# Attention by whole heads with a late division, and part of an output projection moved among the mixers

## The chip, the cores and the metric

The kernel runs on one core of one Trainium2 chip. The metric is the device time of one execution in microseconds. In the profile PE is TensorE's matmul, PEld its weight load, DVE is VectorE, ACT is ScalarE, POOL is GpSimd, SP is SyncE, which issues the DMAs.

## What is computed

Two transformer blocks of two layers each, over 512 tokens of 1024 features, in fp32. Only the second block's token mixing is touched. In one layer of it three mixers read the same normalised input, and their outputs, side by side, go through one output projection:

```python
h = rms_norm_2(x, norm_g[l, 0]) * (1.0 + sc1) + sh1
aq, ak, av, bq, bff, bfb, bi, bg, cq, ck, cv = jnp.split(h @ w_in[l], split_idx, axis=-1)
o_a = mixer_a(...)            # softmax attention, 6 heads of 64, 2 key heads
o_b = mixer_b(...)            # gated linear recurrence in both directions, 4 heads
o_c = mixer_c(...)            # attention with a bias by distance, 6 heads, 2 key heads
mix = jnp.concatenate([o_a, o_b, o_c], axis=-1) @ w_out[l]     # 384 + 256 + 384 -> 1024
x = x + g1 * mix
h = rms_norm_2(x, norm_g[l, 1]) * (1.0 + sc2) + sh2
x = x + g2 * conv_ffn(h, ...)
```

An attention head's output is `softmax(q k^T) v`: exponentials of the scores, divided by their row sums, times the values.

## The kernel before, in words

Activations lie with features on the partitions: a tensor of 1024 features by 512 tokens is eight tiles of 128 x 512. Each weight matrix is cut into tiles of 128 output features. To keep fp32 precision, a product is done as three matmuls on rounded halves (high x high, high x low, low x high): `wload` fetches a raw weight tile, ScalarE rounds it (`wh`, L141), VectorE takes the remainder (`wl`, L146), and `mm3` (L186) issues the three. Two buffers each hold the raw, the high and the low weights.

The mixers of one layer are Python generators, each of which yields an estimate of its TensorE time. `weave` draws from several of them: the next step comes from the stream with the smallest ratio of time so far to its weight. That gives each instruction its place in the program; a scheduler with a timeline simulation then orders each engine's instructions by readiness and that place. At run time every engine works in the order so fixed.

Mixer a and mixer c are attentions. `attn2_unit` takes two blocks of 128 queries of one head: scores for 512 keys (`s`, L1267), a pass of VectorE that copies them to `E` and takes the row maximum (L1376, L1438), ScalarE's exponential with the row sum (L1380, L1444), the reciprocal of the sums (L1383, L1445), and `normalise` (L607), which scales every row of `E`. Then `pv_out` transposes `E` by 128 x 128 blocks into PSUM (`pt`, L595), ScalarE copies that to `pT` (L597), and the product with the values is collected in `pv` (L600), the two query blocks in two halves of the partitions, each instruction 128 columns wide. VectorE copies it to `y` (L603). Two heads share one tile `y`.

Mixer b goes by pairs of heads. `b_levels` builds a triangular 512 x 512 matrix in nine levels of doubling block size: products of VectorE (`zz`, L1571, and `Y`, L1526), exponentials on ScalarE, a running sum on GpSimd (L1530), and small matmuls (`lv`, L1503, L1550, L1558). `b_out` multiplies it by the values (`pvb`), `b_norm` and `b_gate` finish.

A first `weave` runs b's first preparation beside a's. A second runs `b_levels(0)` beside a's attentions and c's first preparation. A third runs pair 1 of b, c's attentions (weight 22) and a chain of b's output, c's remaining preparation, b's norms and gates (weight 28). `room` marks the end of that chain: only from there on are finished `y` rounded into `oh` and `ol` (`mix_done`), since the tiles they take are in use until the last input projection.

Then `block2` loads the residual `x` from DRAM (L1774), where it was put before the mixers, and does the output projection: for each of eight output tiles a weight tile of 1024 columns and 24 matmuls over the eight tiles of `oh`, `ol` (`residual`, L1726, adds to `x`). The first three output tiles are done over 512 tokens, the last five first over tokens 0 to 255, then, as cover for the next norm, over tokens 256 to 511. The norm's chain is: squares on ScalarE, sums on VectorE, a column sum on TensorE (`stat`, L234), an inverse root in eleven small steps on GpSimd (L206 to L224), a broadcast by TensorE (`stat`, L239), scaling, and the two halves `hh` and `hl`. The feed-forward part (`up`) follows.

Of the kernel before, what the change touches and what calls it, by code (L numbers as in the profile page):

```python
# [16 lines left out]
P = 128  # L17
# [86 lines left out]
class Kern:  # L104
# [1153 lines left out]
    def attn2_unit(self, q, ks, v, kv, soft, finish, y, row, i0):  # L1258


        nc = self.nc
        es = []
        for j in range(2):
            i = i0 + j
# [4 lines left out]
            soft(s, i, j, e)  # L1269
# [97 lines left out]
    def a_units(self):  # L1367
        nc = self.nc
        for h in range(6):
            if h % 2 == 0:  # L1370
                y = self.b2("y")
            for i0 in (0, 2):
                mx, nm, sm, rc = (self.small(2) for _ in range(4))

                def soft(ps, i, j, e):
                    nc.vector.tensor_tensor_reduce(e, ps, bc(self.zero[:, 0:1], S), op0=ALU.add, op1=ALU.max, scale=1.0,  # L1376
                                                   scalar=-3e38, accum_out=mx[:, j:j + 1])
                    c = 8 * (h // 2) + 2 * i + h % 2
                    nc.vector.tensor_tensor(nm[:, j:j + 1], mx[:, j:j + 1], self.ansc[:, c:c + 1], op=ALU.mult)
                    nc.scalar.activation(e, e, AF.Exp, bias=nm[:, j:j + 1], scale=self.asc[:, c:c + 1], accum_out=sm[:, j:j + 1])  # L1380
# [6 lines left out]
                self.attn2_unit(self.aqs[h], self.aks[h // 3], self.va, h // 3, soft, finish, y, (h % 2) * 64, i0)  # L1387
                yield 2.6
            if h % 2:
                self.y2[h // 2] = y  # L1390
# [34 lines left out]
    def c_units(self):  # L1425
        nc = self.nc
        for h in range(6):
# [4 lines left out]
            if h % 2 == 0:  # L1432
                y = self.b2("y")
            for i0 in (0, 2):
                mx, nm, sm, rc = (self.small(2) for _ in range(4))

                def soft(ps, i, j, e):
                    nc.vector.tensor_tensor_reduce(e, ps, tb[:, 384 - P * i:896 - P * i], op0=ALU.add, op1=ALU.max, scale=1.0,  # L1438
                                                   scalar=-3e38, accum_out=mx[:, j:j + 1])

                def finish(es):
                    nc.vector.tensor_scalar(nm, mx, -1.0, None, op0=ALU.mult)
                    for j, e in enumerate(es):
                        nc.scalar.activation(e, e, AF.Exp, bias=nm[:, j:j + 1], accum_out=sm[:, j:j + 1])  # L1444
                    nc.vector.reciprocal(rc, sm)  # L1445
                    for j, e in enumerate(es):
                        self.normalise(e, rc[:, j:j + 1])

                self.attn2_unit(self.cqs[h], self.cks[h // 3], self.cva, h // 3, soft, finish, y, (h % 2) * 64, i0)
                yield 2.6  # L1450
            if h % 2:
                self.mix_done(5 + h // 2, y)
# [182 lines left out]
    def mixers(self):  # L1635
# [277 lines left out]
```

## Time and profile before

| | us |
|---|---|
| median of 3 runs | 3018.26 (3018.15 to 3021.32) |
| the profiled execution | 3018.07 |
| its span | 3016.3 |
| TensorE busy | 2910.5 (96%) |
| VectorE busy | 1921.0 (64%) |
| ScalarE busy | 1351.2 (45%) |
| chain that ended last: share on TensorE | 83% |

The span runs from the first to the last instruction of the profile. Busy time of TensorE counts each matmul from its issue to its modelled end, and matmuls overlap, so a busy TensorE isn't one that works at its peak. Stages of one layer repeat in the other: the second block's first layer lies at about 1650 to 2310 us, its second from there to the end.

### The profile page before, as it was taken

To read this page: it belongs to the slowest core of one execution; us is meant where nothing else is said; L and a number is where in the kernel's file an instruction comes from. 1 tells how busy PE (TensorE), PEld (TensorE's weight loads), DVE (VectorE), ACT (ScalarE), POOL (GpSimd) and SP (SyncE) were. 2 spreads that over 40 slices of the span, in tenths; PEclk is the share of its full clock that TensorE was granted. 3 is DMA by queue.
4 is the path that set the end of the run, shared out by engine and by line. 5 is a ranking of instruction groups with operands and counts; after the bars stand their busy time and mean duration, and the time that the engine had idled before them with its cause. 6 is when DMAs were issued, how large, how long until landed. Compare 5 with 4: busy or idle time off the path is not lost.

```text
span 3016.3 us, 46253 instructions
## 1 busy us (share of the span) xinstructions
PE 2910.5 (96%) x17942; PEld 2415.4 (80%) x17942; DVE 1921.0 (64%) x3731; ACT 1351.2 (45%) x2417; POOL 249.8 (8%) x492
## 2 busy tenths in 40 slices
PE   7999999999998999999999999999999998999999
PEld 5888888888887888777778776788888876788887
DVE  5565655555556566665666777688853788576642
ACT  3445454322235345653225675544433676454421
POOL 0000000001112000000112222000000223000000
PEclk9999999999998999999999998999999999999999
DMA  6221111333342323124664211355543311232233
GB/s 228 87 67 60 48 63 64 121 127 120 119 161 84 125 83 107 52 69 169 222 216 134 70 50 47 99 175 196 203 144 109 103 43 60 79 105 98 98 102 95
DMA packets 113164, 331.77 MB, mean 110 GB/s; under 512 B 18160, under 2 KB 20720, under 8 KB 112944
## 3 DMA queue, kind: packets, MB, share of 16 engines
q1 hardware_dynamic: 112944, 328.81, 32.9%
q8 instruction: 141, 2.31, 0.3%
q14 instruction: 79, 0.65, 0.1%
HBM read 300.51 MB, written 17.76 MB: 106 GB/s over the span
## 4 chain that ended last, share of the span: by engine, by line
PE 83%; DVE 8%; ACT 2%; issue 1%; DMA 1%; POOL 1%; SPq 0%; DVEq 0%; ACTq 0%; POOLq 0%
PE mm L186 31%; PE up L186 15%; PE dn L186 10%; PE pu L186 5%; PE pv L600 4%; PE pt L595 4%; PE po L186 3%; PE s L907 2%; PE pre L186 1%; PE s L624 1%; PE s L1267 1%; DVE zz L1571 1%; DVE wl L146 1%; PE pq L186 1%; DVE E L607 1%
## 5 line engine op out<-in xcount | busy, mean ns | idle before, releaser
L146 DVE TENSOR_TENSOR wl<-wraw,wh 128x512 fp32r<-128x512 f32 x704 | 472.4, 710 | 389.2 <-ACT wh L141 385.7
L141 ACT CAST wh<-wraw 128x1024 fp32r<-128x1024 f32 (+4 forms) x363 | 364.9, 1005 | 741.0 <-PE mm L186 227.4
L186 PE MATMUL mm<-hh,wh 128*128 128x512 f32 (+1 forms) x1232 | 483.5, 396 | 11.1 <-ACT wh L141 4.0
L186 PE MATMUL mm<-hl,wh 128*128 128x512 f32 (+1 forms) x1232 | 486.1, 395 | 0.0
L186 PE MATMUL mm<-hh,wl 128*128 128x512 f32 (+1 forms) x1232 | 484.9, 394 | 0.2
L186 PEld LDWEIGHTS mm<-hh,wh 128*128 128x128 f32 x1232 | 233.5, 191 | 59.8 <-ACT wh L141 6.7
L186 PEld LDWEIGHTS mm<-hh,wl 128*128 128x128 f32 x1232 | 234.4, 190 | 49.3 <-DVE wl L146 3.0
L186 PEld LDWEIGHTS mm<-hl,wh 128*128 128x128 f32 x1232 | 234.8, 191 | 46.8 <-issue 2.9
L186 PE MATMUL up<-hh,wh 128*128 128x512 f32 (+1 forms) x688 | 260.8, 381 | 3.4 <-ACT wh L141 2.1
L186 PE MATMUL up<-hh,wl 128*128 128x512 f32 (+1 forms) x688 | 261.1, 380 | 0.2 <-DVE wl L146 0.2
L186 PE MATMUL up<-hl,wh 128*128 128x512 f32 (+1 forms) x688 | 260.7, 380 | 0.5 <-DVE hl L352 0.2
L597 ACT COPY pT<-pt 128x512 f32<-128x512 f32 (+1 forms) x304 | 158.8, 551 | 176.6 <-PE pt L595 175.3
L283 DVE SCALAR_TENSOR_TENSOR macc<-mw,sc,macc 128x1024 f32<-128x1024 f32 x140 | 181.7, 1313 | 70.7 <-DMA mw<-w_mod 37.5
L595 PE MATMUL pt<-ident,E 128*128 128x128 f32 x1120 | 174.6, 282 | 4.7 <-DVE E L607 4.2
L595 PEld LDWEIGHTS pt<-ident,E 128*128 128x128 f32 x1120 | 127.2, 141 | 37.3 <-issue 25.7
L186 PEld LDWEIGHTS up<-hh,wh 128*128 128x128 f32 x688 | 128.9, 188 | 29.1 <-ACT wh L141 2.5
L186 PEld LDWEIGHTS up<-hl,wh 128*128 128x128 f32 x688 | 129.1, 188 | 26.3 <-DVE hl L352 1.1
L186 PEld LDWEIGHTS up<-hh,wl 128*128 128x128 f32 x688 | 129.2, 188 | 25.5 <-issue 0.8
L1020 POOL TENSOR_TENSOR m<-m,gt 128x768 f32<-128x768 f32 (+1 forms) x32 | 55.1, 1721 | 1084.3 <-DVE gt L1016 755.6
L186 PE MATMUL mm<-ch,wh 128*128 128x256 f32 x496 | 141.8, 286 | 0.1
L186 PE MATMUL mm<-ch,wl 128*128 128x256 f32 x496 | 141.6, 286 | 0.0
L186 PE MATMUL mm<-cl,wh 128*128 128x256 f32 x496 | 141.3, 285 | 0.0
(442 smaller groups left out, 6129.6 us busy)
## 6 DMA issues: line engine op xcount, KB each, us to landing
wraw<-w_in SPq DMA_DIRECT2D x158, 512.0 KB, 3.5
mw<-w_ada SPq DMA_DIRECT2D x96, 512.0 KB, 4.3
wraw<-w_up SPq DMA_DIRECT2D x88, 512.0 KB, 3.5
mw<-w_mod SPq DMA_DIRECT2D x32, 512.0 KB, 3.6
wraw<-w_down SPq DMA_DIRECT2D x32, 512.0 KB, 3.5
wraw<-w_branch SPq DMA_DIRECT2D x24, 512.0 KB, 4.0
wraw<-w_out SPq DMA_DIRECT2D x22, 512.0 KB, 3.4
wraw<-w_o SPq DMA_DIRECT2D x19, 512.0 KB, 4.2
```

What stands on the lines that cost most here:

```text
L141: self.nc.scalar.copy(out, in_)
L146: (eng or self.nc.vector).tensor_tensor(out, in_, hi.bitcast(F32), op=ALU.subtract)
L186: self.last = self.nc.tensor.matmul(ps[: n1 - n0, c0 - o:c1 - o], lhsT=a[:, k, n0:n1], rhs=b[j][:, c0:c1], start=start and i == 0, stop=st ...
L283: nc.vector.scalar_tensor_tensor(acc[r], w, sc[:, k, r:r + 1], acc[r], op0=ALU.mult, op1=ALU.add)
L595: nc.tensor.transpose(pt[:, o * P:o * P + P], ecol(j, kb), self.ident)
L597: nc.scalar.copy(tt[:, :n], pt[:, :n])
L600: nc.tensor.matmul(pv[64 * j:64 * j + 64, :P], lhsT=vst(kb), rhs=tt[:, o * P:o * P + P], start=i == ends[j][0], stop=i == ends[j][-1])
L607: self.nc.vector.tensor_scalar(e, e, r, None, op0=ALU.mult)
L624: nc.tensor.matmul(s[:, c0:c1], lhsT=q[:, i * P:(i + 1) * P], rhs=kp[:, a0:a0 + c1 - c0], start=pi == 0, stop=pi == 1)
L907: self.nc.tensor.matmul(ps, lhsT=a[:96, i * P:(i + 1) * P], rhs=b[:96, c0:c1], start=pi == 0, stop=pi == 2)
L1020: nc.gpsimd.tensor_tensor(ms[n][:, :tn], ms[n][:, :tn], m[:, :tn], op=ALU.add)
L1267: nc.tensor.matmul(s, lhsT=q[:, i * P:(i + 1) * P], rhs=kp, start=pi == 0, stop=pi == 1)
```

## The change

The attentions of the second block go by whole heads. `attn2_head` computes the scores of all four query blocks of a head, and no longer scales `E`. For each block of 128 keys it transposes four 128 x 128 blocks, copies 512 columns at once, and issues the product with 256 columns for each half of the partitions. The row sums' reciprocals of a pair of heads are kept (`rc`), and when the pair is complete `divide` spreads them over 64 features (`rx`), transposes that into PSUM (`hr`) and multiplies `y` by it.

`w_out_a` is a new stream step at the end of the third chain, whose weight goes from 28 to 45. For each of eight output tiles it loads the residual into a tile `xa` (tag `t`, four buffers, shared with the squares, spreads and copies of the mixers), loads the 384 weight columns that belong to mixer a, does nine matmuls over 512 tokens, adds, and stores the residual back to DRAM. The projection behind the mixers then has five of eight input tiles, with weight tiles of 640 columns and 15 matmuls.

```diff
-    def attn2_unit(self, q, ks, v, kv, soft, finish, y, row, i0):
+    def attn2_head(self, q, ks, v, kv, soft, finish, y, row):
...
-        self.pv_out([(kb, [0, 1]) for kb in range(4)], lambda j, kb: es[j][:, kb * P:(kb + 1) * P],
-                    lambda kb: v[:, kb, kv, :], y, row, i0 * P)
+        yield 2.0
+        pv = self.ps1("pv", "pv")
+        for kb in range(4):
+            pt = self.ps1("pt", "pt")
+            for i in range(4):
+                nc.tensor.transpose(pt[:, i * P:i * P + P], es[i][:, kb * P:kb * P + P], self.ident)
+            tt = self.ptp.tile([P, 512], F32, tag="pT", name=self.nm("pT"), bufs=3)
+            nc.scalar.copy(tt, pt)
+            for j in range(2):
+                nc.tensor.matmul(pv[64 * j:64 * j + 64, :256], lhsT=v[:, kb, kv, :], rhs=tt[:, 256 * j:256 * j + 256],
+                                 start=kb == 0, stop=kb == 3)
+        for j in range(2):
+            nc.vector.tensor_copy(y[row:row + 64, 256 * j:256 * j + 256], pv[64 * j:64 * j + 64, :256])
+        yield 3.2
+
+    def divide(self, y, r):
+        rr = self.head_rows(r, 0, 2, 64)
+        self.nc.vector.tensor_tensor(y, y, rr, op=ALU.mult)
...
-                def finish(es):
-                    nc.vector.reciprocal(rc, sm)
-                    for j, e in enumerate(es):
-                        self.normalise(e, rc[:, j:j + 1])
...
+            yield from self.attn2_head(self.aqs[h], self.aks[h // 3], self.va, h // 3, soft,
+                                       lambda es: nc.vector.reciprocal(r[:, :, h % 2], sm), y, (h % 2) * 64)
             if h % 2:
+                self.divide(y, r)
...
+    def w_out_a(self, xd, mod):
+        nc = self.nc
+        oy = [self.oh[i] for i in range(3)], [self.ol[i] for i in range(3)]
+        for n in range(KD):
+            x = self.b2("t", name="xa")
+            nc.sync.dma_start(x, xd[n])
+            w = self.wload(self.A["w_out_2"][self.l, n][:, :3 * P], 3, P)
+            ps = self.ps1("dn")
+            self.mm3(ps, w, oy, [(0, S)])
+            nc.vector.scalar_tensor_tensor(x, ps, mod[:, 16 + n, 0:1], x, op0=ALU.mult, op1=ALU.add)
+            nc.sync.dma_start(xd[n], x)
+            yield 2.1
...
-                       (self.chain(self.b_out(0), ..., self.room()), 28.0))
+                       (self.chain(self.b_out(0), ..., self.room(), self.w_out_a(xd, mod)), 45.0))
...
-                    ks = [(k, k) for k in (0, 1, 2, 5, 6, 3, 4, 7)]
+                    ks = [(k - 3, k) for k in (5, 6, 3, 4, 7)]
...
-                        w = self.wload(A["w_out_2"][l, n], KD, P)
+                        w = self.wload(A["w_out_2"][l, n][:, 3 * P:], 5, P)
```

The lines of the changed kernel lie up to 19 further down. On VectorE in the first layer, among the levels of pair 0 and the heads of mixer a, the order before has a reciprocal, the next scores, and then the scaling of two blocks (`sm` are small columns):

```order
L1383 RECIPROCAL sm_16688<-sm_16687 128x2
L1376 ISA E_16766,sm_16759<-s_16763,zero 128x512
L1376 ISA sm_16759 128x1
L1376 ISA E_16773,sm_16759<-s_16770,zero 128x512
L1376 ISA sm_16759 128x1
L1571 TENSOR_TENSOR zz_16177<-bq_16443,ez_17121 64x512 x2
L607 TENSOR_SCALAR E_16692<-E_16692,sm_16688 128x512
L607 TENSOR_SCALAR E_16699<-E_16699,sm_16688 128x512
```

With the change the same place has the scores of a head, one reciprocal for four blocks, and the division of a finished pair:

```order
L1391 ISA E_16980,mx_16960<-s_16977,zero 128x512
L1391 ISA mx_16960 128x1
L1398 RECIPROCAL rc_16832<-su_16835 128x4
L1289 TENSOR_TENSOR y_16510<-y_16510,hr_16823 128x512
L1391 ISA E_16987,mx_16960<-s_16984,zero 128x512
L1391 ISA mx_16960 128x1
L1394 TENSOR_TENSOR nm_16961<-mx_16960,ans_16403 128x1
L1531 TENSOR_TENSOR Y_17368<-f_3039_16183,ey_17371 128x512
```

The scaling of `E` is gone from between the exponentials and the transposes; `y` is scaled instead, once per pair.

On TensorE, at a level of pair 1 in the first layer, input projections (`mm`) followed before:

```order
L1503 MATMUL lv_18159<-zz_16176,Y_18149 32x64 x16
L600 MATMUL pv_17742<-pT_17759,va_3255_17113 64x128 x4
L186 MATMUL mm_18222<-hh_15558,wh_18223 128x512
L186 MATMUL mm_18222<-hl_15559,wh_18223 128x512
L186 MATMUL mm_18222<-hh_15558,wl_18224 128x512
L186 MATMUL mm_18222<-hh_15563,wh_18223 128x512
```

Now the projections stand earlier, and mixer a's share of the output projection (`dn`) follows there:

```order
L1280 MATMUL pv_18065<-pT_18098,va_3239_17046 64x256 x2
L1508 MATMUL lv_18170<-zz_16177,Y_18160 32x64 x16
L186 MATMUL dn_18216<-oh_18192,wh_18210 128x512
L186 MATMUL dn_18216<-ol_18193,wh_18210 128x512
L186 MATMUL dn_18216<-oh_18192,wl_18211 128x512
L186 MATMUL dn_18216<-oh_18196,wh_18210 128x512
```

Of the 72 such matmuls of a layer, 27 stand before pair 1's last level, the others between it and the last two heads.

On SyncE's queue, in the first layer, the loads of the residual (`xa<-xm`), its stores (`xm<-xa`) and the weights stand like this, where before there were only weights and the biases `tb`:

```order
L1651 DMA xm_3033_16156<-xa_18208 128x512
L166 DMA wraw_18467<-w_out 128x384
L1646 DMA xa_18463<-xm_3033_16156 128x512
L1651 DMA xm_3033_16156<-xa_18280 128x512
L166 DMA wraw_18512<-w_out 128x384
L1651 DMA xm_3033_16156<-xa_18352 128x512
L166 DMA wraw_18540<-w_out 128x384
```

The fifth load stands behind the first store, whose tile it takes over.

## Rows read from the trace of the kernel before

**Rows 1.** The page, part 1: busy us, share of the span, instructions.
```profile
PE 2910.5 (96%) x17942; PEld 2415.4 (80%) x17942; DVE 1921.0 (64%) x3731; ACT 1351.2 (45%) x2417; POOL 249.8 (8%) x492
```
**Rows 2.** Windows, first layer, A to F: stretch, length, busy us (count) by engine, clock, DMA.
```profile
1708.00:1769.40 61.40, 56.66 (x529) 40.93 (x528) 54.44 (x136) 40.97 (x83) 23.76 (x43) 0.97 0.14 45
1769.40:1817.60 48.20, 48.20 (x292) 39.14 (x290) 30.40 (x77) 36.12 (x61) 3.44 (x3) 1.00 0.22 67
1817.60:1877.90 60.30, 54.94 (x510) 39.28 (x510) 49.12 (x115) 34.77 (x72) 22.18 (x43) 0.83 0.13 42
1877.90:1904.50 26.60, 26.11 (x164) 19.04 (x163) 16.47 (x43) 14.33 (x30) 3.05 (x11) 1.00 0.12 38
1904.50:1919.90 15.40, 11.63 (x110) 8.49 (x108) 9.77 (x30) 8.46 (x20) 0.00 (x0) 1.00 0.47 142
1919.90:1961.30 41.40, 41.33 (x289) 38.34 (x289) 24.81 (x49) 21.67 (x41) 2.96 (x11) 0.96 0.35 115
sum 253.30, PE 238.86 PEld 185.22 DVE 185.00 ACT 156.33 POOL 55.38; mean PE 39.81 PEld 30.87 DVE 30.83 ACT 26.06 POOL 9.23
```
**Rows 3.** Windows, second layer: the sum of the same six stages, 2391.6 to 2647.2.
```profile
sum 255.60, PE 238.50 PEld 184.06 DVE 191.64 ACT 160.19 POOL 52.97; mean PE 39.75 PEld 30.68 DVE 31.94 ACT 26.70 POOL 8.83
```
**Rows 4.** Timeline of PE at 1791.6 us: start, duration, line, operation, count.
```profile
1791.69 0.39 PE L186 MATMUL mm<-hh,wh 128*128 128x512 f32 x1
1791.92 0.39 PE L186 MATMUL mm<-hl,wh 128*128 128x512 f32 x1
1792.24 1.09 PE L600 MATMUL pv<-pT,va 128*64 128x128 f32 x16
1793.26 1.09 PE L595 MATMUL pt<-ident,E 128*128 128x128 f32 x8
1794.11 0.47 PE L186 MATMUL mm<-hh,wl 128*128 128x512 f32 x1
```
**Rows 5.** Timeline of PE at 1946 us, the output projection at half width.
```profile
1946.95 0.28 PE L186 MATMUL dn<-oh,wl 128*128 128x256 f32 x1
1947.07 0.28 PE L186 MATMUL dn<-oh,wh 128*128 128x256 f32 x1
```
**Rows 6.** DVE's groups by form, 1640 to 2010 us: count, busy us, mean ns, idle before.
```profile
L607 DVE TENSOR_SCALAR E<-E,sm 128x512 f32<-128x512 f32 x48 | 21.9, 499 | 0.4
...
L603 DVE COPY y<-pv 64x128 f32<-64x128 f32 x48 | 13.8, 287 | 4.8 <-PE pv L600 4.3
...
L1239 DVE COPY rx<-sm 128x512 f32<-128x512 f32 x7 | 3.0, 424 | 3.5 <-POOL sm L224 3.4
...
L1402 DVE TENSOR_TENSOR nc<-nc,hr 128x512 f32<-128x512 f32 x4 | 2.7, 687 | 0.1
```
**Rows 7.** DVE's waits in A, first layer: us in total, times, longest.
```profile
DVE sm L1383 <- ACT E L1380: 4.3, 2, 2.1
```
**Rows 8.** DVE's waits in C, first layer.
```profile
DVE sm L1445 <- ACT E L1444: 5.6, 5, 2.2
```
**Rows 9.** Timeline of PE at 1919.9 us, the first matmul after the last head.
```profile
1919.88 0.73 PE L186 MATMUL dn<-oh,wh 128*128 128x512 f32 x2 [1.86 <-ACT oh L141]
```
**Rows 10.** Timeline, 1951 to 1962 us: the norm's chain behind the output projection.
```profile
1951.51 0.50 PE L234 MATMUL stat<-ones,sq 128*128 128x1 f32 x4
...
1955.90 0.20 POOL L224 TENSOR_TENSOR sm<-sm,sm 128x2 f32<-128x2 f32 x1
...
1958.07 0.38 PE L239 MATMUL stat<-ident,sm 128*128 128x128 f32 x2
...
1961.29 0.28 PE L186 MATMUL up<-hh,wh 128*128 128x256 f32 x1
```
**Rows 11.** DMA issues: tensor, count, KB each, median us from issue to landing.
```profile
wraw<-w_out SPq DMA_DIRECT2D x22, 512.0 KB, 3.4
...
xm<-x SPq DMA_DIRECT2D x16, 256.0 KB, 2.8
x<-xm SPq DMA_DIRECT2D x16, 256.0 KB, 2.8
```

More of the change, by code (lines that the diff above doesn't have):

```diff
@@ L1254, in values @@
         return v
-    def attn2_unit(self, q, ks, v, kv, soft, finish, y, row, i0):
+    def attn2_head(self, q, ks, v, kv, soft, finish, y, row):
         nc = self.nc
         es = []
-        for j in range(2):
-            i = i0 + j
+        for i in range(4):
             s = self.ps1("s", "s")
@@ L1268, in attn2_unit @@
             e = self.hblk(F32, "E")
-            soft(s, i, j, e)
+            soft(s, i, e)
             es.append(e)
         finish(es)
-        self.pv_out([(kb, [0, 1]) for kb in range(4)], lambda j, kb: es[j][:, kb * P:(kb + 1) * P],
-                    lambda kb: v[:, kb, kv, :], y, row, i0 * P)
+        yield 2.0
+        pv = self.ps1("pv", "pv")
+        for kb in range(4):
+            pt = self.ps1("pt", "pt")
+            for i in range(4):
+                nc.tensor.transpose(pt[:, i * P:i * P + P], es[i][:, kb * P:kb * P + P], self.ident)
[10 more added lines that the diff above has]
+        self.nc.vector.tensor_tensor(y, y, rr, op=ALU.mult)
     def mix_done(self, i, y):
@@ L1370, in a_units, with soft @@
             if h % 2 == 0:
[L1371 to L1380, printed above, removed]
-                def finish(es):
-                    nc.vector.reciprocal(rc, sm)
-                    for j, e in enumerate(es):
-                        self.normalise(e, rc[:, j:j + 1])
-                self.attn2_unit(self.aqs[h], self.aks[h // 3], self.va, h // 3, soft, finish, y, (h % 2) * 64, i0)
-                yield 2.6
+                y, r = self.b2("y"), self.small(8, "rc").rearrange("p (t h) -> p t h", t=4)
+            mx, nm, sm = (self.small(4, t) for t in ("mx", "nm", "su"))
+            def soft(ps, i, e):
+                nc.vector.tensor_tensor_reduce(e, ps, bc(self.zero[:, 0:1], S), op0=ALU.add, op1=ALU.max, scale=1.0,
+                                               scalar=-3e38, accum_out=mx[:, i:i + 1])
+                c = 8 * (h // 2) + 2 * i + h % 2
+                nc.vector.tensor_tensor(nm[:, i:i + 1], mx[:, i:i + 1], self.ansc[:, c:c + 1], op=ALU.mult)
+                nc.scalar.activation(e, e, AF.Exp, bias=nm[:, i:i + 1], scale=self.asc[:, c:c + 1], accum_out=sm[:, i:i + 1])
+            yield from self.attn2_head(self.aqs[h], self.aks[h // 3], self.va, h // 3, soft,
+                                       lambda es: nc.vector.reciprocal(r[:, :, h % 2], sm), y, (h % 2) * 64)
             if h % 2:
+                self.divide(y, r)
                 self.y2[h // 2] = y
@@ L1432, in c_units, with soft @@
             if h % 2 == 0:
[L1433 to L1450, printed above, removed]
+                y, r = self.b2("y"), self.small(8, "rc").rearrange("p (t h) -> p t h", t=4)
+            mx, nm, sm = (self.small(4, t) for t in ("mx", "nm", "su"))
+            def soft(ps, i, e):
+                nc.vector.tensor_tensor_reduce(e, ps, tb[:, 384 - P * i:896 - P * i], op0=ALU.add, op1=ALU.max, scale=1.0,
+                                               scalar=-3e38, accum_out=mx[:, i:i + 1])
+                nc.vector.tensor_scalar(nm[:, i:i + 1], mx[:, i:i + 1], -1.0, None, op0=ALU.mult)
+                nc.scalar.activation(e, e, AF.Exp, bias=nm[:, i:i + 1], accum_out=sm[:, i:i + 1])
+            yield from self.attn2_head(self.cqs[h], self.cks[h // 3], self.cva, h // 3, soft,
+                                       lambda es: nc.vector.reciprocal(r[:, :, h % 2], sm), y, (h % 2) * 64)
             if h % 2:
+                self.divide(y, r)
                 self.mix_done(5 + h // 2, y)
@@ L1654, in mixers @@
             self.weave((self.chain(self.b_prep(1), self.b_levels(1), self.b_out(1), self.b_norm(1)), 40.0), (self.c_units(), 22.0),
-                       (self.chain(self.b_out(0), self.stagger(self.c_prep([1]), self.b_norm(0), self.c_prep([2]), self.b_gate(1), self.b_gate(0)), self.room()), 28.0))
+                       (self.chain(self.b_out(0), self.stagger(self.c_prep([1]), self.b_norm(0), self.c_prep([2]), self.b_gate(1), self.b_gate(0)), self.room(), self.w_out_a(xd, mod)), 45.0))
             self.b_done(0)
@@ L1766, in block2 @@
                         nc.sync.dma_start(xd[n], self.x[n])
-                    self.mixers()
+                    self.mixers(xd, mod)
                     bq.tile([P, 56], F32, tag="pad", name=f"pad{l}")
```

4 lines of the change are left out of this document (2 added, 2 removed).

## The prediction

> **What bounds the kernel now.** I read the page's busy shares first, then the stages of the second block's two layers as windows, then the timeline of TensorE for its pace, and last what VectorE waits for. On the page the reader is to see TensorE busy for 96% of the span [rows 1]: what shortens the run must shorten TensorE's own line. The edits touch only the stretch of each layer from the first attention score to the first matmul of the feed-forward part, 253.3 us in the first layer [rows 2] and 255.6 us in the second [rows 3]. I cut it into six stages: A (levels of pair 0 beside the first mixer's attentions), B (the rest of these beside projections), C (levels of pair 1 beside the third mixer's attentions), D (last projections, first part of the output projection), the tail (last two heads), and F (output projection and norm).
>
> Busy time overstates TensorE there. A 512-column matmul lasts 0.39 us, but the next begins 0.227 us later (1791.69, 1791.92) [rows 4]; a 256-column one begins 0.12 us after the one before [rows 5]. Eight transposes take 0.85 us, sixteen instructions of eight P·V products 1.02 us [rows 4], of which 0.91 is their columns at the pace above (16 × 0.227/4) and 0.11 the change between the two kinds. Counting each stage's instructions in the order and giving them these paces by columns (fp32 four times the columns of the rounded kind, outputs of 64 or 32 partitions two or four abreast), I estimate TensorE's own work as 47.7 of 61.4 us in A, 46.3 of 48.2 in B, 40.3 of 60.3 in C, 24.1 of 26.6 in D, 9.2 of 15.4 in the tail, 38.7 of 41.4 in F. Together 206.4 of 253.3: 46.9 us are lost, 33.7 of them in A and C. In the second layer the same count gives 212.2 of 255.6, with 11.1 lost in A and 20.2 in C. In A and C VectorE is the busiest of the other engines (54.4 of 61.4, 49.1 of 60.3) [rows 2], and 4.3 and 5.6 us of its idle time are reciprocals that wait for ScalarE's exponentials [rows 7, 8] with the next scores queued behind them. C also has a granted clock of 0.83 [rows 2], so part of it ran at the lower of the two levels (1.2 GHz) after gaps in TensorE's work.
>
> The Trainium skill ("Perfetto Trace Analysis", Identifying the Most-Contended Engine) says that matmul busy time is a poor measure of headroom because matmuls overlap, and the trace agrees: by busy time the first layer's stretch has only 253.3 − 238.9 = 14.4 us to win, by the pace of the rows 46.9. By busy time A and C could give at most 4.7 + 5.4 us, and after the costs below the sum would come to about 3017 us; I go by the pace.
>
> **The change part by part**, for one layer, and against the profiled execution (3018.1 us, its span 3016.3 and 1.8 around it; the median of the runs shown is 3018.3, so the two need no correction).
>
> *Division at the end.* Removed: 48 scalings of a score block by 0.48 us or a little more, 21.9 us of VectorE [rows 6]. Added, once per pair of heads, six times: a copy that spreads the reciprocals (0.42, as the rx row), four transposes on TensorE (4 × 0.85/8 = 0.43) and one multiplication with a PSUM operand (0.69, as the nc row): 6.7 us of VectorE, 2.6 us of TensorE. Copies out of PSUM: 48 of 0.287 us become 24 of twice the width; no row has that shape, it lies between 0.287 (fixed cost alone) and 0.574 (twice); I take 0.42, the middle, which frees 3.7 us (0 to 6.9). Reciprocals halve, the third mixer's negated maxima double: nothing. Net, VectorE loses about 19 us.
>
> In A this is worth most, since VectorE sets the pace there. By the order, 14 scalings go before pair 0's last level (14 × 0.50 = 7.0 us), and three more score blocks get through by then (2.1 us at 0.69 each, the price of such a pass over PSUM as in the nc row): about 5 us less. And the reciprocal, now one per head and needed only for the division, is off the way of the transposes; of 4.3 us of waiting I count 4 as gone (0 if VectorE still stops there, because it is in order). A then takes 61.4 − 5 − 2 to 4 = 52.4 to 54.4 us, and holds 49.9 us of TensorE's work. I take a loss of 4.5 us in place of 13.7.
>
> *Whole heads.* The P·V columns are the same (two products of 128 against one of 256), so TensorE's work stays. The two kinds alternate more often (111 changes per layer before, 122 after, by the order), 1.2 us at 0.11 each; most of it falls into B, which now holds 69.9 us of work, as projections have moved up from C and D: loss 3.5 instead of 1.9.
>
> *The first mixer's share of the output projection.* 72 matmuls of 512 columns, 16.3 us, leave F and come into C and D; before, 27 of them were done at that width and 90 at half, 6.1 + 10.8 = 16.9 us, so 0.6 us is saved. With them move eight weight loads of 192 KB in their two halves, eight loads and eight stores of the residual (256 KB each, 2.8 us to land [rows 11]) and eight VectorE multiply-adds. C now holds 32.7 us of TensorE work. On VectorE 12 scalings (6.0 us) and 5 of 13 score blocks (3.5) leave it with some 2.5 us of small instructions, and four remainders of a cast and two multiply-adds come in (6 × 0.69 = 4.1): 8 us less, 41 instead of 49.1. At VectorE's old share C ends after 60.3 × 41/49.1 = 50.4 us; without the 5.6 us of waits for reciprocals after 45. I take 47.7, the middle: a loss of 15 (12 to 18) for 20.0. D, filled by the new matmuls, loses 2.5 as before.
>
> *The tail* waits longer at its end: after the last product come the copy, the new 0.69 us multiplication and only then the cast for which TensorE waited 1.86 us [rows 9]. Loss 7 for 6.2.
>
> *F* has 25.9 us of work instead of 38.7 and so less cover. From the column sums (1951.51) to the row broadcast (1958.07) the order gave 51 half-width matmuls, then 25 more until the first feed-forward matmul at 1961.29 [rows 10]. Now it is 30 and none. The chain itself needs 1955.90 + 0.20 − 1951.51 = 4.6 us to the end of the root, and from the broadcast to the first finished operand 3.2 us with ScalarE's cast in between, perhaps 1.6 without. Cover is 30 × 0.12 = 3.6: 1 us bare at the root, 1.6 to 3.2 behind it, and 1 to 2 at the second half's column sums, which now stand only eight matmuls later. The weights of a half-width tile must also come every 15 × 0.12 = 1.8 us instead of 2.9, through two buffers with 3.4 us to landing for the old size [rows 11]; I add 1 to 3 us. F's loss, 2.7 before, becomes 6 with what shows behind it (3 to 12).
>
> *Sum.* First layer: own work 206.4 + 2.6 − 0.6 = 208.4; losses 4.5 + 3.5 + 15 + 2.5 + 7 + 6 = 38.5 for 46.9. Change: 2.0 − 8.4 = −6.4. Second layer: A and C lost 11.1 + 20.2 there, 2.4 less than in the first, so its change is about −4.0. Together −10.4: 3018.1 − 10.4, about 3008 us.
>
> **The rivals.** *Nothing much changes.* In C the levels' own chain (VectorE, ScalarE, GpSimd in turn) and not VectorE's load sets the end, and C keeps its loss of 20, D included. For it: GpSimd and ScalarE are far from full there, yet TensorE waits. Against it: VectorE at 49.1 of 60.3. Then 2 × 5 us are missing: about 3018, with a part of them some 3015 (3011 to 3020).
>
> *The filler works fully.* TensorE always finds output-projection matmuls between the levels, the clock stays at its upper level and C loses 8. Then 2 × 7 us more: 2994. For it: B, where such matmuls lie between the same attentions, loses 1.9 of 48.2. Against it: in the order only 27 of the 72 stand before pair 1's last level.
>
> *The residual's round trip makes it slower.* One mechanism: the new tile shares four buffers with others, and by the order its fifth to eighth load can be issued only when an earlier one's store has landed. SyncE's queue is in order, and the weights of later columns stand behind these loads. Place: D. Price: up to four stops of 2.8 us [rows 11] in each layer, 22 us in all, less what is hidden: a column's matmuls take 9 × 0.227 = 2.0 us, so from about half of each stop on it shows. If all of it shows, 3008 + 22 = 3030; it decides (slower than 3024) from three of four. Against it: weights are asked for three or four columns ahead. The Trainium skill ("DMA: Bandwidth & Descriptors", on where the fixed 2 us go) warns that completion is slowest for writes to HBM. The rows do not bear this out, store and load both land in 2.8 us; by the skill's rule this rival would be dearer than by the row, and I keep the row.
>
> **How the numbers follow.** The forecast (3001 to 3013) has 0.45, no change 0.27, the full filler 0.15, slower 0.13. The range should hold eight of ten: from 2994, the full filler, to 3021, beyond no change. What a measurement can tell from no change is 0.2%, 6 us: faster means below 3012.2, slower above 3024.3. Faster takes nearly all of the forecast, the filler and some of the no-change case (0.43 + 0.15 + 0.05), same 0.25, slower 0.12.
>
> **What would show it.** In the profile after: no scaling of a score block in the second block, and VectorE's wait for reciprocals nearly gone; A near 54 us with VectorE still over 85% busy; C near 48 with output-projection matmuls between its last levels; idle of 1 to 3 us each before the broadcast and before the first feed-forward matmuls; 72 full-width output-projection matmuls ahead of the last two heads. The prediction is wrong if A does not shorten, if TensorE waits for weights in D, or if F's bare norm exceeds 6 us a layer.

## The result, and the profile after

The changed kernel takes 3034.58 us (median of 6 runs, 3030.64 to 3037.18) against 3018.2 (3017.4 to 3021.32): a ratio of 1.0052, interval 1.0039 to 1.0065. The forecast was 3008, with a range of 2994 to 3021: the change made the kernel slower by 16 us where 10 us less were forecast. The profiled execution took 3030.64 us, its span is 3028.9, so the traces differ by 12.6 us.

The page after, part 1, answers [rows 1]: TensorE's busy share is the same, with 2 us more of it.

```profile
PE 2912.5 (96%) x17516; PEld 2388.5 (79%) x17516; DVE 1898.3 (63%) x3643; ACT 1359.6 (45%) x2433; POOL 252.8 (8%) x492
```

The windows of the same six stages (start and end, length, busy us and count of PE, PEld, DVE, ACT, POOL, granted clock, DMA share, GB/s); B reaches to the first level of pair 1, C to its last. The second sum is that of the second layer, 2395.3 to 2658.7 us:

```profile
1706.70:1766.40 59.70, 56.19 (x498) 38.95 (x497) 54.05 (x128) 45.23 (x92) 22.89 (x43) 1.00 0.15 48
1766.40:1840.60 74.20, 74.20 (x393) 54.11 (x391) 34.23 (x86) 44.55 (x76) 7.86 (x20) 1.00 0.18 55
1840.60:1890.30 49.70, 39.77 (x406) 27.05 (x406) 45.46 (x90) 32.57 (x66) 16.78 (x27) 0.90 0.22 72
1890.30:1916.00 25.70, 23.55 (x110) 14.20 (x109) 12.10 (x24) 6.84 (x12) 2.24 (x11) 1.00 0.53 164
1916.00:1933.60 17.60, 13.22 (x81) 7.30 (x79) 8.32 (x31) 11.43 (x27) 0.00 (x0) 1.00 0.30 109
1933.60:1966.20 32.60, 29.13 (x190) 25.90 (x190) 22.02 (x52) 20.24 (x45) 2.90 (x11) 0.95 0.32 103
sum 259.50, PE 236.06 PEld 167.52 DVE 176.17 ACT 160.87 POOL 52.68; mean PE 39.34 PEld 27.92 DVE 29.36 ACT 26.81 POOL 8.78
...
sum 263.40, PE 242.81 PEld 172.75 DVE 179.37 ACT 163.97 POOL 53.96; mean PE 40.47 PEld 28.79 DVE 29.89 ACT 27.33 POOL 8.99
```

Against [rows 2, 3] the first layer's stretch is 6.2 us longer, the second's 7.8; all the rest of the program is 1.4 us shorter. Take the sums apart into TensorE's busy and idle time. First layer: busy 238.9 before, 236.1 now; idle 14.4 before, 23.4 now. Second layer: busy 238.5 and 242.8, idle 17.1 and 20.6. Of the 14.0 us in the two layers 12.5 are idle time of TensorE. In the first layer it has gone up in C (5.4 to 9.9), in D (0.5 to 2.2), a little in the tail (3.8 to 4.4) and in F (0.1 to 3.5), and down only in A (4.7 to 3.5). B, 26 us longer, has none: it holds work that stood in C and D before. (TensorE's busy time isn't all work at full pace; a table at the end of the experiments takes it apart.)

The largest waits of TensorE after, first layer (us in total, times, longest):

```profile
PE pt L1276 <- DVE nc L1413: 5.7, 1, 5.7
PE dn L186 <- ACT oh L141: 5.0, 2, 2.9
PE up L186 <- ACT hh L351: 2.3, 1, 2.3
```

The first is in C and new. TensorE's timeline there (start, duration, line, operation, the idle time before it):

```profile
1854.48 0.50 PE L1266 MATMUL s<-kh,qa 128*128 128x512 f32 x1
1854.82 0.39 PE L1266 MATMUL s<-kl,qa 128*128 128x512 f32 x1
1855.05 0.60 PE L1241 MATMUL hr<-ident,rx 128*128 128x128 f32 x4
1861.37 1.54 PE L1276 MATMUL pt<-ident,E 128*128 128x128 f32 x6 [5.72 <-DVE nc L1413]
```

`hr` and `pt` share two PSUM tiles. Two `hr` (one of a division, one of a query's scaling) hold both until VectorE, which works in order, comes to them; TensorE's next transposes wait 5.7 us, and in the second layer as long. The other two are the end of the tail and the bare norm in F:

```profile
1914.22 0.74 PE L186 MATMUL dn<-oh,wh 128*128 128x512 f32 x2 [2.15 <-ACT oh L141]
...
1933.62 1.04 PE L186 MATMUL dn<-oh,wh 128*128 128x512 f32 x2 [2.85 <-ACT oh L141]
...
1963.47 0.43 PE L239 MATMUL stat<-ident,sm 128*128 128x128 f32 x2 [0.61 <-POOL sm L224]
1966.17 0.38 PE L186 MATMUL up<-hh,wh 128*128 128x256 f32 x1 [2.27 <-ACT hh L351]
```

The row of 1.86 us [rows 9] is 2.85 now, and the broadcast and the first feed-forward matmul [rows 10], which nothing held up before, wait 0.61 and 2.27 us.

### The profile page after: what moved, and what is told of

Read it like the earlier page. It is cut to its first block, busy times and chain, and to the rows that moved or that the text cites. A ratio compares the mean times of both kernels' runs of the same rounds, so it can differ in the third digit from the quotient of the medians.

```text
span 3028.9 us, 45408 instructions
## 1 busy us (share of the span) xinstructions
PE 2912.5 (96%) x17516; PEld 2388.5 (79%) x17516; DVE 1898.3 (63%) x3643; ACT 1359.6 (45%) x2433; POOL 252.8 (8%) x492
## 4 chain that ended last, share of the span: by engine, by line
PE 84%; DVE 7%; ACT 2%; DMA 1%; issue 1%; POOL 1%; SPq 0%; DVEq 0%; ACTq 0%; POOLq 0%
PE mm L186 31%; PE up L186 16%; PE dn L186 10%; PE pu L186 5%; PE pv L600 3%; PE po L186 3%; PE pt L595 3%; PE s L907 2%; PE pv L1280 1%; PE pre L186 1%; PE s L1266 1%; PE s L624 1%; PE pt L1276 1%; DVE zz L1576 1%; DVE wl L146 1%
## 5 line engine op out<-in xcount | busy, mean ns | idle before, releaser
L146 DVE TENSOR_TENSOR wl<-wraw,wh 128x512 fp32r<-128x512 f32 (+1 forms) x720 | 471.9, 694 | 388.7 <-ACT wh L141 386.3
L141 ACT CAST wh<-wraw 128x1024 fp32r<-128x1024 f32 (+5 forms) x379 | 366.7, 968 | 743.3 <-PE mm L186 223.5
L597 ACT COPY pT<-pt 128x512 f32<-128x512 f32 (+1 forms) x208 | 105.8, 537 | 145.2 <-PE pt L595 144.3
L186 PE MATMUL dn<-ah,wl 128*128 128x512 f32 (+1 forms) x358 | 136.5, 381 | 0.0
L186 PE MATMUL dn<-al,wh 128*128 128x512 f32 (+1 forms) x358 | 136.4, 381 | 0.0
```

Source lines behind the costliest of these rows:

```text
L141: self.nc.scalar.copy(out, in_)
L146: (eng or self.nc.vector).tensor_tensor(out, in_, hi.bitcast(F32), op=ALU.subtract)
L186: self.last = self.nc.tensor.matmul(ps[: n1 - n0, c0 - o:c1 - o], lhsT=a[:, k, n0:n1], rhs=b[j][:, c0:c1], start=start and i == 0, stop=st ...
L597: nc.scalar.copy(tt[:, :n], pt[:, :n])
```

## Experiments

All times are medians, with the ratio to the kernel before in the same session and its interval. The stages are those of the first layer unless another is named.

### One half of the change at a time

e1 takes the heads and the late division alone, e2 the share of the output projection alone. e3 and e4 keep the whole change and touch the division.

```diff
 e1: - ... self.room(), self.w_out_a(xd, mod)), 45.0)
     + ... self.room()), 28.0)
     - ks = [(k - 3, k) for k in (5, 6, 3, 4, 7)]
     + ks = [(k, k) for k in (0, 1, 2, 5, 6, 3, 4, 7)]
     ...
 e2: the kernel before with w_out_a and weight 45
 e3: - rr = self.head_rows(r, 0, 2, 64)
     + rr = self.head_rows(r, 0, 2, 64, 'mm')
     ...
 e4: - self.divide(y, r)
```

> Attentions by whole heads with the late division, the output projection left whole behind the mixers as before, third chain's weight 28. Theory P (PSUM): the division's broadcast tile takes one of the two PSUM tiles that the heads' transposes need, and TensorE stops until VectorE reaches it (5.7 us in each layer's stretch C of the changed kernel). Then this half of the change alone is slower than before: F keeps its cover (41 us), A gains 1 to 4 us, C pays 5 to 8 us a layer: 3022 to 3030. Theory O (output projection): the heads are neutral or a small gain and the moved projection is what costs: 3008 to 3018.

> The first mixer's share of the output projection among the mixers (third chain's weight 45), the attentions as before. Theory P: no broadcast tile of a division is there, so no 5.7 us stop; the filler shortens F by 9 us and lengthens what lies before it by about as much: 3012 to 3022. Theory O: the moved loads, stores and VectorE additions cost what the changed kernel loses, 3026 to 3036.

> The changed kernel, but the broadcast of the reciprocals for the division goes into one of the three PSUM tiles of the projections instead of one of the two of the transposes. Theory P: the stop of 5.7 us a layer shrinks to under 1.5 us and the run comes to 3020 to 3026. Theory O: it stays at 3031 to 3037, the stop moves to another place.

> The changed kernel without the division (reciprocals are computed, the spread, its transposes and the multiplication are left out, so the attention outputs stay undivided). It bounds what the division costs with all its waits. Theory P: its own work is 1.3 us of TensorE and 3.4 us of VectorE a layer, the rest is the stop: 3014 to 3022. Theory O: only its own work goes, 3028 to 3033.

e1: 3017.44, ratio 1.0003 (0.9992 to 1.0013), no difference. e2: 3043.1, 1.0091 (1.0074 to 1.0109). e3: 3054.7, 1.0127 (1.0108 to 1.0146). e4: 3030.14, 1.005 (1.0033 to 1.0067). Theory P's ranges miss all four times. Theory O's hold e1 and e4, while e2 and e3 lie above both: the loss comes with the projection, whose share came with the weight of 45. With share and weight in place the heads even help: e2, without them, takes 8 us more than the changed kernel. The 5.7 us stop is real, but it is not what makes C long: without any division (e4) C takes 48.9 us and TensorE still idles 9.7 of them, behind other waits. e3 doesn't isolate the stop: with the broadcast in another PSUM tile the stop is gone, but the whole order turns over, and A, with 86 transposes in it for 48, grew to 77.8 us.

The windows of e1, with D and the tail in one row:

```profile
1707.40:1767.10 59.70, 56.16 (x498) 39.00 (x497) 54.06 (x128) 45.17 (x92) 22.91 (x43) 1.00 0.16 48
1767.10:1819.20 52.10, 52.10 (x280) 39.28 (x281) 28.52 (x68) 35.35 (x58) 4.11 (x3) 1.00 0.24 68
1819.20:1875.00 55.80, 48.23 (x442) 30.77 (x442) 43.31 (x91) 34.84 (x71) 23.03 (x43) 0.88 0.15 45
1875.00:1916.60 41.60, 37.92 (x215) 23.72 (x213) 22.04 (x55) 20.89 (x43) 3.41 (x11) 1.00 0.20 66
1916.60:1958.00 41.40, 41.32 (x288) 38.38 (x289) 25.19 (x49) 21.96 (x41) 2.96 (x11) 0.96 0.38 115
sum 250.60, PE 235.73 PEld 171.15 DVE 173.11 ACT 158.20 POOL 56.42; mean PE 47.15 PEld 34.23 DVE 34.62 ACT 31.64 POOL 11.28
```

A is the same to a tenth as in the changed kernel: what the heads do to A they do alone. Everything else differs from there on: B 52.1 for 74.2, idle 14.9 in all for 23.4.

### The weight or the share

The share came with a weight of 45 for its chain. e5 is the changed kernel with 28, e6 is e1 with 45, e7 takes the residual's loads and stores away, e8 the whole step at weight 45.

```diff
 e5: - self.w_out_a(xd, mod)), 45.0)
     + self.w_out_a(xd, mod)), 28.0)
 e6: - self.room()), 28.0)
     + self.room()), 45.0)
 e7: - nc.sync.dma_start(x, xd[n])
     - nc.vector.scalar_tensor_tensor(x, ps, mod[:, 16 + n, 0:1], x, op0=ALU.mult, op1=ALU.add)
     - nc.sync.dma_start(xd[n], x)
     + nc.vector.tensor_scalar(x, ps, mod[:, 16 + n, 0:1], None, op0=ALU.mult)
 e8: - self.room(), self.w_out_a(xd, mod)), 45.0)
     + self.room()), 45.0)
```

> The changed kernel with the third chain's weight back at 28. Theory W (weight): at 45 the third chain is drawn ahead of pair 1's preparation, so that 22 us of its projections stand before pair 1's first level (it starts 74 us after pair 0's last level instead of 52 in the kernel with the heads alone), and the levels, a chain that takes about 50 us whatever lies beside it, end later by that. Then B comes back to 50 to 60 us and the run to 3012 to 3024. Theory S (share): it is the share's own matmuls, loads and VectorE additions that cost: 3028 to 3037, the time moves from B to D.

> Heads and late division alone, output projection whole, but the third chain's weight at 45. Theory W: B 70 to 76 us instead of 52, C 42 to 50 instead of 56, since the projections that filled it are gone: 3026 to 3042. Theory S: no share, so no cost: 3012 to 3021.

> The changed kernel without the residual's round trip: the share's product is scaled on VectorE and neither is the residual loaded nor the sum stored (so the first mixer's share is missing in the output). Round trip as the cause (the rival of the prediction): the stops of the weights behind these transfers go, 3014 to 3026. Theories W and S, which do without it: 3029 to 3037.

> The changed kernel with weight 45 but without the step of the share (its loads, 72 matmuls of a layer, additions and stores are left out). Theory W: the share fills idle time of TensorE in part only, the order of B is what costs; 3010 to 3022, with B still 72 to 76 us. Theory S: all of its 16.3 us of matmuls a layer and more is exposed, 2995 to 3004.

e5: 3020.14, 1.001 (0.9999 to 1.002). e6: 3049.24, 1.011 (1.0094 to 1.0125). e7: 3033.54, 1.0058 (1.0044 to 1.0072). e8: 3021.47, 1.0014 (1.0004 to 1.0025). The rival of the round trip is out: without it the run is as long. Theory S's ranges miss e5, e6 and e8; theory W's hold e5 and e8, and e6 lies 7 us above its own. With e1 and the changed kernel, e5 and e6 make a square of medians:

| heads and late division, with | weight 28 | weight 45 |
|---|---|---|
| projection whole | 3017.4 | 3049.2 |
| share among the mixers | 3020.1 | 3034.6 |

At weight 45 the share gives 15 us back; the weight takes 32, or 14 with the share. At 28 the share is worth nothing (3 us, inside the spread of the runs; the kernel before gave medians from 3015.4 to 3018.2 beside the different experiments). C and the row of D and tail in e6, and the sums of e6 and e8:

```profile
1841.70:1894.40 52.70, 37.95 (x383) 23.64 (x382) 43.00 (x85) 31.97 (x64) 17.11 (x27) 0.81 0.09 29
1894.40:1934.30 39.90, 30.25 (x159) 18.04 (x158) 14.06 (x42) 14.37 (x32) 2.22 (x11) 0.91 0.18 53
...
sum 267.80, PE 239.76 PEld 173.07 DVE 171.30 ACT 158.48 POOL 53.00; mean PE 47.95 PEld 34.61 DVE 34.26 ACT 31.70 POOL 10.60
```

```profile
sum 256.10, PE 223.69 PEld 158.10 DVE 169.01 ACT 157.81 POOL 53.51; mean PE 44.74 PEld 31.62 DVE 33.80 ACT 31.56 POOL 10.70
```

By the order, weight 45 puts 192 matmuls of projections ahead of pair 1's first level where 28 puts 144. C then has nothing to lay beside the levels: TensorE idles 14.8 us in it instead of 7.6, and 9.7 instead of 3.7 behind it, and the granted clock is 0.81 (e1: 0.88). VectorE's load in C is the same, 43 us. The share is a filler for the hole that its own weight opened: from e8 to the changed kernel TensorE's busy time in the first layer rises by 12.4 us and the idle time falls by 9.0.

### Does the place of the levels decide?

Theory W also said why: the levels of pair 1 start 22 us later. e9 to e11 put them back with the share left in, by a larger weight for pair 1's chain.

```diff
 e9:  - self.b_norm(1)), 40.0), (self.c_units(), 22.0)
      + self.b_norm(1)), 64.0), (self.c_units(), 22.0)
 e10: 50.0 and 22.0      e11: 64.0 and 30.0
```

> The changed kernel, but pair 1's chain gets weight 64 instead of 40, so that it and the third chain (45) stand to each other as 40 to 28 before; the third mixer's attentions stay at 22. Theory W: by the order two projections fewer (144 matmuls instead of 192) stand before pair 1's first level; B 50 to 54, C 51 to 55 with 8 score blocks in it instead of 10, the share's matmuls nearly all in D: 3012 to 3024. If the weight only moves the loss to D and F, 3028 to 3036.

> The same with 50 in place of 64: by the order one of the two projections comes back (168 matmuls). Theory W as a dose: B 62 to 68, between 52 and 74, C 49 to 53, the run between the two, 3020 to 3031. If B's order isn't the cause, 3031 to 3037 like the changed kernel.

> As the kernel with weights 64, 22 and 45, but the third mixer's attentions at 30: 12 score blocks in C, 6 left for D. Theory W: B 50 to 54, 3012 to 3024. Since VectorE's load sets C (42 to 45 us busy in every version so far), C is 2 to 5 us longer than with 22, D shorter by as much.

e9: 3041.41, 1.0081 (1.0069 to 1.0094). e10: 3036.36, 1.0067 (1.0055 to 1.008). e11: 3038.43, 1.0073 (1.006 to 1.0087). All three miss theory W's ranges, and with them that half of it falls; e10 lies in the range of the other case (3031 to 3037), e9 above it. B, C, the row of D and tail, and the sum in e9:

```profile
1770.40:1823.00 52.60, 52.60 (x284) 39.78 (x283) 28.76 (x69) 34.80 (x57) 5.33 (x9) 1.00 0.21 61
1823.00:1878.10 55.10, 44.53 (x415) 27.73 (x414) 42.55 (x80) 32.21 (x64) 20.05 (x37) 0.88 0.08 25
1878.10:1938.70 60.60, 55.52 (x293) 36.01 (x292) 31.66 (x80) 27.81 (x59) 2.56 (x11) 0.99 0.46 152
...
sum 261.70, PE 239.20 PEld 169.41 DVE 178.75 ACT 160.03 POOL 53.88; mean PE 47.84 PEld 33.88 DVE 35.75 ACT 32.01 POOL 10.78
```

B came back to 52.6 as forecast (65.9 in e10, 52.1 in e11), and the run grew. B's length was a displacement, not a loss: TensorE never idles in it. The idle time in the stages where levels and heads wait stayed: e9 has 22.5 us of it in the first layer, the changed kernel 23.4, e1 14.9. The projections are back in C (25 matmuls, one in the changed kernel, 26 in e1), but 16 score matmuls stand there where e1 and the changed kernel have 20. Idle time alone doesn't explain why e9 is 7 us slower than the changed kernel; the table below does.

### What sets A

e12 is e1 with a short pass of VectorE over the first mixer's scores, which are also scaled by a tenth.

```diff
- nc.vector.tensor_tensor_reduce(e, ps, bc(self.zero[:, 0:1], S), ...
+ nc.vector.tensor_tensor_reduce(e[:, :64], ps[:, :64], bc(self.zero[:, 0:1], 64), ...
- nc.scalar.activation(e, e, AF.Exp, ...
+ nc.scalar.activation(e, ps, AF.Exp, ...
...
```

> What sets A: heads and late division alone (weight 28, projection whole), but in the first mixer the pass over the scores reads only 64 of 512 columns (about 0.15 us instead of 0.69), the exponential reads the scores from PSUM, and the scores are scaled by a tenth so that it stays finite: the softmax is another one. 17 to 20 score blocks in A, so 9 to 11 us less of VectorE there. If VectorE's load sets A (the prediction's step): A 50 to 55 instead of 59.7, 57 to 60 instead of 63.6, the run 3000 to 3010. If the levels' own chain sets it: A within 1.5 us of 59.7 and 63.6, the run 3011 to 3018.

3016.9, 1.0006 (0.9997 to 1.0015), no difference. Its stage A in the windows:

```profile
1707.40:1764.60 57.20, 53.31 (x476) 36.73 (x475) 43.51 (x114) 41.47 (x84) 23.93 (x43) 1.00 0.16 48
```

VectorE's largest wait in it:

```profile
DVE E L1391 <- PE s L1266: 8.1, 4, 5.0
```

VectorE lost 10.6 us in A, and A only 2.5 (in the second layer 3.2). A got shorter by what left TensorE: 17 score blocks stand in it for 20, and 2.9 us of TensorE's busy time went with them. The work appears further on: B is 52.3 us for 52.1, D with the tail 44.1 for 41.6. VectorE now stands idle for 8.1 us, waiting for TensorE's scores. So VectorE's load does not set A, and the other theory's 1.5 us were exceeded too. That TensorE sets A, which neither theory had named, is read from its busy time (53.3 of 57.2 here, 56.2 of 59.7 in the changed kernel); no run lightened TensorE alone to show it.

### The cover of the norm, and other weights

e13 and e14 give F its cover back, in the changed kernel and in that with weight 28; e15 and e16 are e1 with other weights.

```diff
 e13, e14: - if n < KD - 5:
           + if n < KD - 8:
           ...
 e15: - self.room()), 28.0)          + self.room()), 20.0)
 e16: - (self.c_units(), 22.0)       + (self.c_units(), 18.0)
```

> The changed kernel (weight 45), but all eight output tiles of the projection behind the mixers, not five, are done in two halves, so that 75 half-width matmuls stand behind the first column sums again (32 before the broadcast, 43 behind it; in the changed kernel 30 and none). Theory F (cover): of TensorE's 3.5 and 3.1 us of idle in F, 2 to 3 us a layer go, against 0.6 us for halving three more tiles and six more weight loads: 3 to 5 us faster than the changed kernel, 3029 to 3032. Theory T (transfers): the extra weight loads eat it up: within 1.5 us of it, 3033 to 3037.

> The same with the third chain's weight back at 28, where C and what follows idle 2 to 5 us less in each layer. Theory F: 3 to 5 us faster than with weight 28 alone (3020): 3014 to 3018, level with the kernel before. Theory T: 3018 to 3023. If idle time of TensorE is what counts (12.2 and 14.8 us a layer before, about 17 with weight 28, about 14 with cover), it can't beat the kernel before by more than 6 us.

> Heads and late division alone, output projection whole, the third chain's weight at 20 instead of 28. By the order 120 projection matmuls stand in B instead of 144, 24 more behind it, and pair 1's levels start 10 us of work earlier. Theory I (idle): what counts is TensorE's idle time beside the levels and the last heads (14.9 us in the first layer with 28, 28.0 with 45); if leaving projections for later goes on paying, 10 to 13 us a layer and 3008 to 3014. If 28 already stands at the best place, C has more score blocks (14 for 10), VectorE is its bound and the run is 3017 to 3026.

> Heads and late division alone with the third mixer's attentions at 18 instead of 22: by the order 12 score blocks in C for 10 and 6 behind it for 8. Theory I: idle time of TensorE in C falls by 1 to 2 us a layer, behind it too: 3011 to 3016. If VectorE's load in C (43 us of 56) sets its end, C grows by 1.5 to 3 us and nothing is won: 3016 to 3021.

e13: 3041.66, 1.009 (1.0076 to 1.0105). e14: 3028.29, 1.0046 (1.0031 to 1.006). e15: 3027.58, 1.0029 (1.0018 to 1.0041). e16: 3032.48, 1.0051 (1.0038 to 1.0063). By the medians all four are slower than the kernel they vary, by 7, 8, 10 and 15 us; neither theory F nor T had said so much, and e15 and e16 are slower than either of their two cases. TensorE's waits in F of e13:

```profile
PE dn L186 <- DVE wl L146: 1.2, 4, 0.6
PE dn L186 <- ACT wh L141: 0.9, 2, 0.5
...
PE stat L239 <- POOL sm L224: 0.3, 1, 0.3
```

The bare norm is gone (2.27 us behind the broadcast, 0.3 left of 0.6 ahead of it), and in its place TensorE waits for rounded weights, since a half-width tile of 15 matmuls uses them up in 1.8 us. F is 35.0 us long (38.7 in the second layer) where the changed kernel's is 32.6 (32.7). But those waits are not why e13 is slower: in the two layers together TensorE's idle time is 1.9 us less than in the changed kernel, and its busy time 8.6 us more.

Part of the busy time is time at the lower of the two granted clocks (0.50, or 1.2 of 2.4 GHz). C of the kernel before shows it, with 1836.6 to 1848.6 us at 0.50 and 1850 to 1860 us at 1.00:

```profile
1836.60:1848.60 12.00, 12.00 (x113) 9.40 (x113) 9.61 (x22) 5.43 (x12) 6.30 (x15) 0.50 0.07 27
1850.00:1860.00 10.00, 10.00 (x136) 7.95 (x134) 7.38 (x13) 7.03 (x14) 6.10 (x13) 1.00 0.15 54
```

```profile
1847.29 0.63 PE L186 MATMUL mm<-hh,wh 128*128 128x512 f32 x1
1847.72 0.63 PE L186 MATMUL mm<-hl,wh 128*128 128x512 f32 x1
...
1850.23 0.40 PE L186 MATMUL mm<-hh,wl 128*128 128x512 f32 x1
1850.46 0.40 PE L186 MATMUL mm<-hh,wh 128*128 128x512 f32 x1
```

The same matmuls begin 0.43 us apart in the first stretch and 0.23 in the second, so by an estimate from these rows 0.47 of the busy time at 0.50 is lost. Windows of half a microsecond over the stages of both layers, added up (us; the last two columns rest on the estimate):

| | length | idle | busy at 0.50 | lost to it | rest of busy |
|---|---|---|---|---|---|
| before | 508.9 | 31.5 | 40 | 19 | 459 |
| e1 | 505.4 | 29.1 | 24 | 11 | 465 |
| e5 | 509.3 | 34.5 | 22 | 10 | 465 |
| the changed kernel | 522.9 | 44.0 | 22 | 10 | 469 |
| e6 | 538.8 | 53.0 | 40 | 19 | 467 |
| e9 | 529.7 | 45.1 | 35 | 16 | 468 |
| e13 | 529.6 | 42.1 | 36 | 17 | 471 |
| e15 | 520.3 | 35.9 | 45 | 21 | 463 |
| e16 | 519.0 | 37.1 | 33 | 15 | 466 |

With the heads in, the rest stays within 8 us while the length varies by 33: idle time and the lower clock make the difference. From e5 to the changed kernel, and from e1 to e6, it is mostly idle time; e9 and e13 lose 6 to 7 us more to the clock than the changed kernel, which is about what they are slower. In D of e13 the clock is 0.50 from 1912.5 to 1918 us, behind a wait of 1.72 us for a rounded `oh`; the changed kernel, with 2.15 us at that place, stays at 1.00. The heads themselves (e1 against the kernel before) added some 6 us of other busy time in the two layers and took 8 from what the clock costs.

In e1 the weights 22 and 28 stand at a place from which each step that was tried costs 8 us or more (e15 by its ratio, 10 by the medians; e16 15, e6 32). No version beats the kernel before by more than the measurement can tell; e1, e5 and e12 are level with it.

## Why the prediction was wrong

**The step that failed is the first: "Busy time overstates TensorE there".** I priced TensorE's instructions at the pace of long rows of equal matmuls and called all beyond it a loss (46.9 us). The timeline of A in the changed kernel shows what that price leaves out:

```profile
1717.13 0.50 PE L1266 MATMUL s<-kh,qa 128*128 128x512 f32 x1
1717.47 0.40 PE L1266 MATMUL s<-kl,qa 128*128 128x512 f32 x1
1717.80 0.63 PE L1508 MATMUL lv<-zz,Y 128*32 128x64 f32 x26
1718.36 0.50 PE L1266 MATMUL s<-kh,qa 128*128 128x512 f32 x1
```

No bracket, so no wait that the profile shows; yet two scores take 0.67 us (1717.13 to 1717.80), where 2 × 0.227 makes 0.45. The changes of kind before and behind such a pair cost 0.2 us, and in A and C the kind changes after every few instructions. Counted by starts, A's 40 scores took 11.7 us where I had 9.1; all of A was busy for 56.2 us where I had 49.9 of work. B shows the same: 74.2 us without one wait, with 69.9 of work by the price (and 73.4 in all by the forecast, which allowed 3.5 of loss). Before the change, TensorE idled 14.4 of the 46.9 us that I called lost in the first layer, and some 12 went to the lower clock by the estimate above. The other 20 are neither, changes of kind are part of them, and no version won them back: in the changed kernel the same remainder is 23. The reading by busy time that I had weighed and set aside gave about 3017, nearer than the forecast. The Trainium skill ("Perfetto Trace Analysis", Identifying the Most-Contended Engine) says that matmul busy time is not a good measure of how close a kernel is to its roofline. The part at the lower clock bears that out here; but the distance to an ideal pace wasn't time that a faster VectorE could win.

The other step that failed is the price of the weight: the prediction let projections that "have moved up from C and D" stand in B and left C's end to VectorE's load. By medians the 26 us between forecast and result are the gain of 10 that did not come (the heads alone took 3017.4 for 3018.2), 3 for the share at weight 28, within the spread (e5), and 14 for the weight of 45. In the first layer's sum the stages missed by 5.3 (A), 0.8 (B), 2.0 (C), 3.8 (D and tail) and 0.7 us (F). None of the three signs named as proof of an error came: A did get shorter, by 1.7 us, TensorE waited 0.6 us for rounded weights in the whole stretch, and F's bare norm took 2.9.

**A**: 59.7 us, forecast 52.4 to 54.4 (the sum took 54.4). Some groups of VectorE's operations in A by form (count, busy us, mean ns, idle before), before and after, show why its load hardly fell, from 54.4 to 54.1:

```profile
L1571 DVE TENSOR_TENSOR zz<-bq,ez 64x512 f32<-64x512 f32 x16 | 11.9, 745 | 0.1
L1376 DVE CUSTOM_DVE_ANT_0 E<-s,zero 128x512 f32<-128x512 f32 x16 | 10.6, 683 | 0.1
L607 DVE TENSOR_SCALAR E<-E,sm 128x512 f32<-128x512 f32 x14 | 6.9, 537 | 0.0
```

```profile
L1391 DVE CUSTOM_DVE_ANT_0 E<-s,zero 128x512 f32<-128x512 f32 x20 | 13.5, 686 | 1.8 <-PE pt L1276 1.2 <-PE s L1266 0.5
L1576 DVE TENSOR_TENSOR zz<-bq,ez 64x512 f32<-64x512 f32 x16 | 13.2, 827 | 0.1
...
L1283 DVE COPY y<-pv 64x256 f32<-64x256 f32 x6 | 2.5, 418 | 0.0
```

6.9 us of scalings went; 2.9 came back in four more score blocks, 1.3 in `zz` (827 ns each, 745 before), the rest in pieces of the third mixer's preparation and the division. The waits for reciprocals [rows 7] did go, and A still gave only 1.7 us. e12 shows that less load would not have mattered much either: 10.6 us less of it gave 2.5.

**B and C** together: 123.9 us, forecast 73.4 + 47.7 = 121.1. C holds 9.9 us of TensorE's idle time for 5.4: the step that scaled C by VectorE's load left out what TensorE has to lay beside the levels once the projections stand in B (where I had counted them), and it did not see the two PSUM tiles.

**D and the tail** together: 43.3 us, forecast 39.5 (30.0 of work and 9.5 of loss). They idle for 6.5, of which 2.15 are a wait for the last product of the second pair that the prediction hadn't named; at weight 28 (e5) it isn't there. **F**: 32.6 for 31.9; its two bare places measured 0.61 and 2.27 where 1 and 1.6 to 3.2 had been forecast. F was right in mechanism and nearly in size, and at weight 28 its two waits (0.6, 2.2) are still there.

**The division's prices** were right: `rx` 425 ns, the multiplication 678 ns (0.69), the copy of twice the width 420 ns (0.42, the middle). Without any division (e4) the run is 4 us shorter, inside the two intervals.

**The rivals.** That nothing much changes (0.27) is true of the heads alone, for another reason than the one given. The full filler (0.15) failed as its counter-argument said: 27 of the 72 matmuls stand in C. The slower case (0.13) got the sign by luck and not the mechanism: the round trip costs nothing (e7). The mechanism that made the kernel slower, a weight that moves TensorE's filler out of the stages that need it, was in the diff and in the order, and no rival named it: I priced it only as a displacement.

**What stays open.** The rows show how long the clock was at 0.50 in each version, not why a wait is followed by it in one place and not in another. The remainder beyond the price is put down to changes of kind from a few rows only. Nor is it shown which waits in C would be left if both `hr` had tiles of their own: e3 changed the whole order.

## What to carry to other kernels

Before you call TensorE's time beyond an ideal pace a loss, look in its timeline for waits: where rows follow each other without one, TensorE's pace is its own, in these rows slower at each change between kinds of matmul, and a faster neighbour can win the idle time and what a lower granted clock takes, no more. A filler has a place: moving matmuls earlier into a stage in which TensorE is already full takes them from the stages that need them, so count idle time and the granted clock by stage before and after, not the length of stages. A weight that comes along with a change is a change of its own; run the two apart.

## What the runs showed of the hardware

The same `zz` product (64x512, fp32) took 745 ns on VectorE in A before and 827 after, with nothing changed in it; 712 in C before and 812 after. The runs do not show why. A new load of the residual (256 KB) took 3.4 us in the changed kernel and its store 2.1 us, where loads and stores of that size both took 2.8 before [rows 11]:

```profile
xa<-xm SPq DMA_DIRECT2D x16, 256.0 KB, 3.4
xm<-xa SPq DMA_DIRECT2D x16, 256.0 KB, 2.1
```
